# Hybrid NSA and HGRN2 decoder layer: TensorE in a hand-written order through the attention, key blocks two by two

## The chip, the cores and the metric

The kernel runs on one core of a Trainium2 chip. The metric is the device time of one execution in microseconds (us). The core has a matrix engine (TensorE, PE in the profile; PEld are its weight loads), a vector engine (VectorE, DVE), a scalar engine (ScalarE, ACT), GpSimd (POOL) and SyncE (SP), which issues the DMAs. Each engine works through its own instructions in order and waits at semaphores for the others.

## What is computed

One decoder layer for 1024 tokens of width 1024, in float32. The part that matters here is the attention of 8 heads in 2 groups, in query blocks of 128, with three branches whose results are added with gates:

```python
# one query block; R = 4 heads to a group, dh = 64
sc = einsum('bqgrd,bngd->bgrqn', qblk, kc) * scale          # 63 compressed keys
p_cmp = masked_softmax(sc, ...); o_cmp = p_cmp @ vc
ss = einsum('bqgrd,bgqkd->bgrqk', qblk, k_sel) * scale       # selected blocks: 16 of 16, so all earlier keys
p_sel = masked_softmax(ss, ...); o_sel = p_sel @ v_sel
sw = einsum('bqgrd,bkgd->bgrqk', qblk, k_win) * scale        # a window of 512
p_win = masked_softmax(sw, ...); o_win = p_win @ v_win
o = g0 * o_cmp + g1 * o_sel + g2 * o_win
...
x = x + concat(o_nsa, o_hgrn) @ w_out
```

Before it stand a projection and a gated linear recurrence (HGRN2) with 4 heads of its own; after it stands a SwiGLU feed-forward part.

## The kernel before

A product of two float32 operands is made of three reduced-precision ones (`mm3`, lines 117 to 120): each operand is split into a high and a low part by one ACT and one DVE instruction. A tile of the output projection (128 tokens by 512 columns) is 4 such triples, 12 matmuls of 512 columns each (`out_tile`, line 491, before the attention's own functions).

The attention (from line 730) goes through 32 units `(qb, g, b)`: 8 query blocks, 2 groups, and b = 0 for all earlier keys, b = 1 for the window. A unit has two halves. `score` (line 815) makes for each of 4 heads the score rows of the query block against all keys of the unit (PE, lines 839 to 842), their maximum (DVE, line 847), the exponential with its sum (ACT, 848), the reciprocal (DVE, 849) and the scaling (POOL, 850). `values` (line 853) goes through the unit's key blocks: 4 transposes of 128 columns bring a block of the weights into PSUM (line 861), ACT and DVE split it into `ph` (863, 864), and two matmuls of 512 columns add it to the output bank (865, 866). After b = 1, `finish` adds the compressed branch in the same way (872 to 879), folds the halves together (ACT 885 and 886, DVE 887 and 888) and writes the result over the queries. The program calls `score` of one unit ahead of `values` of the unit before it.

`prep` (line 773) serves one query block ahead: POOL scales the queries (775), 8 transposes bring both groups into two PSUM banks (781), ACT and DVE empty each into `q` (784, 785), 16 small matmuls and 2 mask matmuls make the compressed scores (790, 795), and a short softmax follows (803 to 813).

PSUM in this stage: two banks named T for everything that is transposed (`ps_t`), one bank a0 for the unit's output, one bank a1 for output tiles (`bank_f`), and for scores either four single banks (query blocks 0 to 3) or two pairs (`ps_s`, from block `NARROW` = 4).

Output tiles are called between units by a counter: each unit adds 1 plus its number of key blocks to `load`, and each 6.5 (`FILL`) pays for one tile, 12 of the HGRN half first (`hq`), then those of the attention half (`nq`). `out_half(0)` loads the second half of the weights where the first list is empty.

What sets the order: the kernel is written with the Tile framework, which takes the program in order as a priority and orders every engine's instructions itself, by its own model of durations; what is ready may be taken ahead of what stands earlier in the program and isn't.

Of the kernel before, what the change touches and what calls it, by code (L numbers as in the profile page):

```python
# [8 lines left out]
F32 = mybir.dt.float32  # L9
# [39 lines left out]
def hybrid_layer(ctx: ExitStack, tc: tile.TileContext, x, x_t, par, w_in, k_norm, pos_k, pos_v,  # L49
# [441 lines left out]
    def out_tile(parts, t, n, mh, ml, bank):  # L491
        sl = slice(n * 512, (n + 1) * 512)
        a = bank()
        for c in range(4):
            wh, wl = parts[c]
            mm3(a, mh[:, c * P:(c + 1) * P], ml[:, c * P:(c + 1) * P], wh[:, sl], wl[:, sl], c == 0, c == 3)
        V.tensor_tensor(x1[:, t, sl], a, x1[:, t, sl], op=OP.add)
# [7 lines left out]
    mixed = {}  # L505
# [8 lines left out]
    def hgrn_out(t, n, bank=bank_f):  # L514
        if n == 0 and t:
            mixed[t] = mix_parts(gmix[:, :, t * P:(t + 1) * P])
        out_tile(w_b, t, n, *mixed[t], bank)


    with tc.tile_pool(name="cp", bufs=1) as cp:  # L520
# [166 lines left out]
        mixed[0] = mix_parts(gmix[:, :, 0:P])  # L687
# [42 lines left out]
    with tc.tile_pool(name="at", bufs=1) as at:  # L730
        g_bc = at.tile([P, D], F32, name="g_bc")
        nc.sync.dma_start(g_bc, norm_ffn[0:1, :].broadcast_to([P, D]))
        def nsa_out(t, n):
            if n == 0:
                mixed[t] = mix_parts(qtok[:, t].rearrange("p (c n) -> p c n", c=4))
            out_tile(w_t, t, n, *mixed[t], bank_f)
            if n == 1:
                nc.sync.dma_start(x1_d[t * P:(t + 1) * P, :], x1[:, t, :])
                rs2 = norm_stats(x1[:, t, :], rpage())
                if t == NT - 1:  # L740
                    g_last = rpage()
                    nc.sync.dma_start(g_last, norm_ffn[0:1, :].broadcast_to([P, D]))
                    V.scalar_tensor_tensor(x1[:, t, :], x1[:, t, :], rs2, g_last, op0=OP.mult, op1=OP.mult)
                    return
                A.activation(x1[:, t, :], x1[:, t, :], AF.Copy, scale=rs2)
                G.tensor_tensor(x1[:, t, :], x1[:, t, :], g_bc, op=OP.mult)
                if t >= 4:
                    G.tensor_tensor(x1[:, t, 0:512], x1[:, t, 0:512], x1[:, t - 4, 0:512], op=OP.subtract)
# [23 lines left out]
        def prep(qb):  # L772
# [5 lines left out]
            for g in range(GROUPS):  # L778
# [7 lines left out]
                qs.append(q)  # L786
            sc = bank_s() if qb <= NARROW else ps_s()[:, 0:512]
# [26 lines left out]
            return qs, pc3  # L814

        def score(qb, g, b, qs):
# [4 lines left out]
            res = []  # L821
            for r in range(4):
                h = 4 * g + r
                s = bank_s() if qb < NARROW else ps_s()
# [18 lines left out]
                nm = small.tile([P, 1], F32, name="nm", tag="nm", bufs=4)  # L843
                den = small.tile([P, 1], F32, name="den", tag="den", bufs=4)
                p0 = 1024 * r if b == 0 else 4096 + 640 * r
                pp = pflat[:, p0:p0 + n]
                V.tensor_reduce(nm, sv, axis=AX.XY, op=OP.max, negate=True)  # L847
                A.activation(pp.rearrange("p (i n) -> p i n", i=sv.shape[1]), sv, AF.Exp, bias=nm, accum_out=den)  # L848
                V.reciprocal(den, den)  # L849
                G.tensor_scalar(pp, pp, den, gates[:, qb, h * 3 + 1 + b:h * 3 + 2 + b], op0=OP.mult, op1=OP.mult)  # L850
                res.append(pp)
            return kb0, res

        def values(qb, g, b, kb0, wts, o):
            for kb in range(kb0, qb + 1):
                pt = bank_t()

                i = kb - kb0 if b == 0 or qb < 4 else 0 if kb == kb0 else 1 if kb == qb else kb - kb0 + 1
                c0 = i * P
                for r in range(4):  # L860
                    PE.transpose(pt[:, r * P:(r + 1) * P], wts[r][:, c0:c0 + P], ident)  # L861
# [36 lines left out]
        for i, u in enumerate(units + [None]):  # L898
            scored = None
            if u:  # L900
                qb, g, b = u
                if u == (NARROW, 0, 0):
                    paired_banks()
# [394 lines left out]
```

## Time and profile before

| | us |
|---|---|
| median of 3 runs | 1396.63 (1396.52 to 1396.65) |
| the profiled execution: its own time | 1396.95 |
| its span, first to last instruction | 1395.2 |
| attention, from the first query transposes' inputs to the last output products | 392.7 to 745.8 |
| PE busy over the span | 1366.1 (98%) |
| DVE, ACT, POOL busy over the span | 1034.3, 596.7, 322.2 |

PE's busy time counts each matmul from its start to a modelled end. Matmuls overlap in the engine, so one that starts late can still touch the one before it, and the engine counts as busy. How much work was really done is read from starts: how far apart they are, and how many fall into a stretch.

### The profile page before, as it was taken

The page shows a single profiled execution, that of the slowest core. Times are in us where ns is not written, and L with a number is a line of the kernel's source. Part 1 is how long each engine was busy: PE and PEld are TensorE (multiplying, and loading weights), DVE is VectorE, ACT ScalarE, POOL GpSimd, SP SyncE. Part 2 cuts the span into 40 slices and gives each one's busy share as a digit, 9 for nine tenths or more (in the row PEclk, how much of TensorE's full clock was granted, in tenths as well). Part 3 has the DMA queues.
Part 4 walks back from the last instruction along what each step waited for, and adds up shares of the span by engine and source line. Part 5 has one row for each costly group of instructions (what it writes and reads, how often), then busy time and mean ns, then how long its engine had stood idle before and what let it go on. Part 6 is the DMA issues. An engine that isn't in the chain of part 4 may idle for free.

```text
span 1395.2 us, 19645 instructions
## 1 busy us (share of the span) xinstructions
PE 1366.1 (98%) x7092; PEld 1127.8 (81%) x7092; DVE 1034.3 (74%) x1937; ACT 596.7 (43%) x1153; POOL 322.2 (23%) x297
## 2 busy tenths in 40 slices
PE   9999999999999999999998999999999999999998
PEld 7888888989977777777776788888888888888887
DVE  5317888626688887888867888888888887578764
ACT  7323333323446666566664433333333333444432
POOL 0001111011035443344345533323323320000000
PEclk9999999999999999999999999999999999999999
DMA  8411110111220001000003233333233336998521
GB/s 326 128 46 31 31 31 29 54 31 46 76 106 1 1 1 61 31 16 16 31 17 106 70 112 99 113 114 113 92 113 98 114 98 234 335 327 317 180 94 53
DMA packets 108768, 135.71 MB, mean 97 GB/s; under 512 B 6112, under 2 KB 63872, under 8 KB 108672
## 3 DMA queue, kind: packets, MB, share of 16 engines
q1 hardware_dynamic: 108672, 134.46, 28.6%
q8 instruction: 56, 0.92, 0.3%
q14 instruction: 40, 0.33, 0.1%
HBM read 105.87 MB, written 28.57 MB: 96 GB/s over the span
## 4 chain that ended last, share of the span: by engine, by line
PE 85%; DVE 10%; ACT 2%; issue 1%; POOL 1%; DMA 0%; ACTq 0%; POOLq 0%; DVEq 0%
PE bank L118 9%; PE bank L119 9%; PE bank L120 9%; PE a L118 8%; PE a L120 8%; PE a L119 8%; PE ps_t L120 4%; PE ps_t L119 4%; PE ps_t L118 4%; PE ps_t L861 3%; PE a L865 2%; PE a L866 2%; PE ps_t L375 1%; PE ps_s L839 1%; DVE nm L847 1%
## 5 line engine op out<-in xcount | busy, mean ns | idle before, releaser
L111 ACT ACTIVATE wop<-rpage 128x512 fp32r<-128x512 f32 x132 | 82.7, 630 | 156.8 <-PE bank L120 70.6
L850 POOL TENSOR_SCALAR pbig<-pbig,den,gates 128x640 f32<-128x640 f32 (+7 forms) x128 | 104.0, 817 | 167.0 <-DVE den L849 147.0
L112 DVE TENSOR_TENSOR wop<-rpage,wop 128x512 fp32r<-128x512 f32 x132 | 101.4, 771 | 13.4 <-ACT wop L111 11.3
L864 DVE TENSOR_TENSOR ph<-ps_t,ph 128x512 fp32r<-128x512 f32 x126 | 84.4, 684 | 18.5 <-ACT ph L863 17.6
L863 ACT ACTIVATE ph<-ps_t 128x512 fp32r<-128x512 f32 x126 | 72.7, 595 | 49.6 <-PE ps_t L861 38.7
L861 PE MATMUL ps_t<-ident,pbig 128*128 128x128 f32 x504 | 78.7, 275 | 2.1 <-POOL pbig L850 2.1
L381 POOL TENSOR_TENSOR kp<-kp,fp 128x256 f32<-128x256 f32 x28 | 20.3, 726 | 231.8 <-PE bank L358 180.3
L861 PEld LDWEIGHTS ps_t<-ident,pbig 128*128 128x128 f32 x504 | 61.0, 141 | 11.9 <-POOL pbig L850 3.2
L112 DVE TENSOR_TENSOR wlo<-wraw,whi 128x1024 fp32r<-128x1024 f32 (+2 forms) x27 | 32.0, 1188 | 46.2 <-PE a L120 19.3
L848 ACT ACTIVATE pbig<-ps_s,nm 128x640 f32<-128x640 f32 (+3 forms) x64 | 55.9, 875 | 24.1 <-DVE nm L847 19.0
L118 PE MATMUL bank<-wop 128*128 128x512 f32 x165 | 64.2, 389 | 0.0
L119 PE MATMUL bank<-wop 128*128 128x512 f32 x165 | 64.2, 389 | 0.0
L120 PE MATMUL bank<-wop 128*128 128x512 f32 x165 | 64.2, 389 | 0.0
L1012 POOL TENSOR_TENSOR tmp<-tmp,rpage 128x512 f32<-128x512 f32 x21 | 31.2, 1488 | 139.2 <-DVE wop L112 139.2
L111 ACT ACTIVATE wop<-act_a 128x512 fp32r<-128x512 f32 x48 | 30.3, 631 | 73.8 <-PE bank L120 48.3
L847 DVE TENSOR_REDUCE nm<-ps_s 128x1 f32<-128x640 f32 (+3 forms) x64 | 58.1, 914 | 4.7 <-PE ps_s L842 3.0
L865 PE MATMUL a<-ph,kv 128*128 128x512 f32 x132 | 58.8, 446 | 2.3 <-ACT ph L863 1.6
L866 PE MATMUL a<-ph,kv 128*128 128x512 f32 x132 | 57.5, 435 | 2.9 <-DVE ph L864 2.4
L112 DVE TENSOR_TENSOR wop<-tmp,wop 128x512 fp32r<-128x512 f32 x42 | 43.7, 1039 | 20.6 <-ACT wop L111 19.7
L111 ACT ACTIVATE wop<-tmp 128x512 fp32r<-128x512 f32 x42 | 26.6, 634 | 70.1 <-POOL tmp L1012 37.5
L112 DVE TENSOR_TENSOR wop<-act_a,wop 128x512 fp32r<-128x512 f32 x48 | 33.2, 691 | 30.7 <-ACT wop L111 30.6
L118 PE MATMUL a<-whi,hT_h 128*128 128x256 f32 (+2 forms) x168 | 55.2, 328 | 0.0
(458 smaller groups left out, 4352.3 us busy)
## 6 DMA issues: line engine op xcount, KB each, us to landing
rpage<-in_w_gate_up_dram SPq DMA_DIRECT2D x86, 256.0 KB, 3.1
raws<-in_w_down_dram SPq DMA_DIRECT2D x35, 512.0 KB, 7.5
act_a<-act_d SPq DMA_DIRECT2D x12, 1024.0 KB, 6.1
act_d<-as SPq DMA_DIRECT2D x33, 256.0 KB, 2.2
act_e<-act_d SPq DMA_DIRECT2D x6, 1024.0 KB, 8.2
act_d<-tmp SPq DMA_DIRECT2D x22, 256.0 KB, 2.2
act_d<-th SPq DMA_DIRECT2D x22, 256.0 KB, 2.1
xn<-in_x_dram SPq DMA_DIRECT2D x8, 512.0 KB, 6.0
```

The source lines that it names most:

```text
L111: A.activation(hi, src, AF.Copy)
L112: V.tensor_tensor(lo, src, hi.bitcast(F32), op=OP.subtract)
L118: PE.matmul(o, ah, bh, start=first, stop=False, skip_group_check=chained)
L119: PE.matmul(o, ah, bl, start=False, stop=False, skip_group_check=chained)
L120: PE.matmul(o, al, bh, start=False, stop=last, skip_group_check=chained)
L847: V.tensor_reduce(nm, sv, axis=AX.XY, op=OP.max, negate=True)
L850: G.tensor_scalar(pp, pp, den, gates[:, qb, h * 3 + 1 + b:h * 3 + 2 + b], op0=OP.mult, op1=OP.mult)
L861: PE.transpose(pt[:, r * P:(r + 1) * P], wts[r][:, c0:c0 + P], ident)
L863: A.activation(ph[:, 0], pt, AF.Copy)
L864: V.tensor_tensor(ph[:, 1], pt, ph[:, 0].bitcast(F32), op=OP.subtract)
L865: PE.matmul(o, vst[b][:, kb, g, :], ph[:, 0], start=b == 0 and kb == kb0, stop=False)
L866: PE.matmul(o, vst[b][:, kb, g, :], ph[:, 1], start=False, stop=False)
```

## The change

Within the attention loop PE's instructions keep the order in which the program issues them (`tc.manual_schedule` with PE alone). The other engines are still ordered by the framework. To have an order worth keeping, the work is cut into pieces:

- an output tile becomes 4 pieces of 3 matmuls (`out_pieces`);
- `score` gives back 4 closures, one for each head, with an estimated cost;
- `values` and `finish` give back steps of three parts: `turn` (transposes and splits), `first` and `second` (the two products);
- `run_steps` takes a unit's steps two by two: both `turn`s, then as many heads and pieces as make an equal share of the unit's fills, then `first`, `first`, `second`, `second`;
- the order in a unit is now: steps of the unit before, with this unit's heads and pieces between them;
- `prep` is cut in two: its 8 transposes come ahead of the steps of unit (qb, 1, 1), and the compressed scores are a fifth "head" of that unit (`later_weights`);
- two products of the feed-forward part (`first_pieces`) become fills of the last steps, and the last output tiles come after them.

```diff
-    def out_tile(parts, t, n, mh, ml, bank):
+    def out_pieces(parts, t, n, mix, bank, tail=None):
...
+        def piece(c):
+            def run():
+                if c == 0:
+                    a.append(bank())
+                wh, wl = parts[c]
+                mh, ml = mix
+                mm3(a[0], mh[:, c * P:(c + 1) * P], ml[:, c * P:(c + 1) * P], wh[:, sl], wl[:, sl], c == 0, c == 3)
+                if c == 3:
+                    V.tensor_tensor(x1[:, t, sl], a[0], x1[:, t, sl], op=OP.add)
+                    if tail:
+                        tail()
+            return run
+        return [piece(c) for c in range(4)]
...
                 qs.append(q)
+            return qs, lambda: compressed(qb, qs)
+
+        def compressed(qb, qs):
             sc = bank_s() if qb <= NARROW else ps_s()[:, 0:512]
...
+            cost = 0.16 + 0.9 * max(n, 256) / 1024
+            return kb0, res, [(lambda r=r: head(r), cost) for r in range(4)]
 
         def values(qb, g, b, kb0, wts, o):
-            for kb in range(kb0, qb + 1):
+
+            def step(kb):
+                ph = []
+
+                def turn():
+                    pt = bank_t()
...
+                    for r in range(4):
+                        PE.transpose(pt[:, r * P:(r + 1) * P], wts[r][:, i * P:(i + 1) * P], ident)
+                    ph.append(at.tile([P, 2, 512], F32R, name="ph", tag="ph", bufs=2))
+                    A.activation(ph[0][:, 0], pt, AF.Copy)
+                    V.tensor_tensor(ph[0][:, 1], pt, ph[0][:, 0].bitcast(F32), op=OP.subtract)
+
+                def first():
+                    PE.matmul(o, vst[b][:, kb, g, :], ph[0][:, 0], start=b == 0 and kb == kb0, stop=False)
+
+                def second():
+                    PE.matmul(o, vst[b][:, kb, g, :], ph[0][:, 1], start=False, stop=False)
+                return turn, first, second
+            return [step(kb) for kb in range(kb0, qb + 1)]
...
+        def run_steps(steps, fills):
+
+            pairs = [steps[k:k + 2] for k in range(0, len(steps), 2)]
+            todo, share = list(fills), sum(c for _, c in fills) / max(len(pairs), 1)
+            used = 0.0
+            for k, pair in enumerate(pairs):
+                for turn, _, _ in pair:
+                    turn()
+                while todo and (k == len(pairs) - 1 or used + todo[0][1] / 2 < share * (k + 1)):
+                    used += todo[0][1]
+                    todo.pop(0)[0]()
+                for j in (1, 2):
+                    for st in pair:
+                        if st[j]:
+                            st[j]()
+            for f, _ in todo:
+                f()
...
+        with tc.manual_schedule(engines={mybir.EngineType.PE}):
+            for i, u in enumerate(units + [None]):
+                scored, heads, fills, steps, ahead = None, [], [], [], []
+                if u:
...
+                    kb0, res, heads = score(qb, g, b, prepped[qb][0])
...
+                while load >= FILL:
+                    load -= FILL
+                    if hq:
+                        t, n = hq.pop(0)
+                        if n == 0:
+                            ahead.append(lambda t=t: hgrn_mix(t))
+                        fills += [(f, 0.7) for f in hgrn_pieces(t, n, bank_f, None if hq else half)]
...
+                if i == len(units):
+                    for t in nq:
+                        fills += nsa_fills(*t)
+                    nq = []
+                    for f in range(2):
+                        fills += first_pieces(f)
+                if u and u[1:] == (1, 1) and u[0] + 1 < NT:
+                    prepped[u[0] + 1] = prep(u[0] + 1)
+
+                    def later_weights(q=u[0] + 1):
+                        compr[q] = prepped[q][1]()
+                    heads.append((later_weights, 2.3))
...
+                    steps = values(qb, g, b, kb0, wts, o_bank[g])
+                    if b == 1:
+                        steps.append(finish(qb, g, compr[qb], o_bank[g]))
...
+                for _ in range(EARLY.count(i - len(units))):
...
+                    steps.append((lambda t=b11_t: operand(b11, x1[:, t, 0:512], t, ps_t), None, None))
+                    b11_t += 1
+
+                k = len(heads) > 3 and len(steps) > 4
+                for f in ahead:
+                    f()
+                run_steps(steps, heads[:2] + fills[:1] * k + heads[2:] + fills[k:])
...
+            mixed[NT - 1] = []
+            nsa_mix(NT - 1)
+            for t in nq:
+                for piece in nsa_pieces(*t):
+                    piece()
```

## Rows read from the trace of the kernel before

**Rows 1.** Busy time by stretch: window and length, each engine's busy us (instructions), PEclk.
```profile
392.70:518.00 125.30, 121.81 (x755) 96.82 (x755) 101.72 (x258) 78.87 (x215) 56.79 (x77) 0.99 0.02 5
518.00:745.80 227.80, 219.28 (x1235) 171.18 (x1235) 181.82 (x387) 142.00 (x279) 86.84 (x75) 0.99 0.08 29
597.60:627.60 30.00, 29.55 (x177) 24.00 (x177) 26.25 (x58) 19.80 (x40) 12.59 (x12) 1.00 0.04 18
```
**Rows 2.** Instructions of one line in the attention: count, duration min/median/max, stretch, forms.
```profile
L861 PE MATMUL ps_t<-ident,pbig x504: 270/272/421, 400.8 to 733.3; 128*128 128x128 f32 x168
L861 PE MATMUL ps_s<-ident,pbig x24: 270/272/299, 718.2 to 733.0; 128*128 128x128 f32 x24
L118 PE MATMUL a<-whi,rpage x108: 387/397/775, 394.5 to 744.4; 128*128 128x512 f32 x108
L839 PE MATMUL ps_s<-kv,q x128: 277/388/522, 504.1 to 717.5; 128*128 128x384 f32 x48, 128*128 128x256 f32 x32, 128*128 128x320 f32 x16, 128*128 128x448 f32 x16
L839 PE MATMUL bank<-kv,q x64: 279/380/562, 395.8 to 495.2; 128*128 128x256 f32 x32, 128*128 128x384 f32 x16, 128*128 128x512 f32 x16
```
**Rows 3.** Timeline of PE where nothing waits: start, us, engine, line, operation, tiles, count.
```profile
570.37 0.39 PE L119 MATMUL a<-wlo,rpage 128*128 128x512 f32 x1
570.60 0.39 PE L120 MATMUL a<-whi,rpage 128*128 128x512 f32 x1
...
571.18 0.28 PE L839 MATMUL ps_s<-kv,q 128*128 128x256 f32 x1
571.30 0.28 PE L840 MATMUL ps_s<-kv,q 128*128 128x256 f32 x1
...
571.90 1.04 PE L861 MATMUL ps_t<-ident,pbig 128*128 128x128 f32 x8
572.69 0.48 PE L118 MATMUL a<-whi,rpage 128*128 128x512 f32 x1
```
**Rows 4.** Timeline around the query transposes of block 3, all engines.
```profile
462.77 0.93 PE L781 MATMUL ps_t<-ident,rpage 128*128 128x128 f32 x7
...
463.45 0.48 PE L118 MATMUL a<-whi,rpage 128*128 128x512 f32 x1
...
463.76 1.27 ACT L784 ACTIVATE q<-ps_t,gains 128x512 fp32r<-128x512 f32 x2
...
464.65 1.41 DVE L785 SCALAR_TENSOR_TENSOR q<-ps_t,gains,q 128x512 fp32r<-128x512 f32 x2
```
**Rows 5.** Timeline of one head of block 0, from its mask matmul to its scaled weights.
```profile
400.41 0.23 PE L842 MATMUL bank<-cmask,identb 128*128 128x128 bf16 x1
...
400.67 0.29 DVE L847 TENSOR_REDUCE nm<-bank 128x1 f32<-128x128 f32 x1 [0.31 <-PE bank L842]
...
401.73 1.37 POOL L850 TENSOR_SCALAR pbig<-pbig,den,gates 128x128 f32<-128x128 f32 x3 [1.19 <-DVE den L849]
```
**Rows 6.** Groups by line and form, heads of 640 keys and the block split: count | busy, mean ns.
```profile
L847 DVE TENSOR_REDUCE nm<-ps_s 128x1 f32<-128x640 f32 x40 | 32.2, 813 | 2.7 <-PE ps_s L840 1.4 <-PE ps_s L842 1.1
...
L848 ACT ACTIVATE pbig<-ps_s,nm 128x640 f32<-128x640 f32 x40 | 31.7, 794 | 12.6 <-DVE nm L847 10.7 <-DVE den L849 1.6 <-DVE n_rs L131 0.2
...
L850 POOL TENSOR_SCALAR pbig<-pbig,den,gates 128x640 f32<-128x640 f32 x40 | 37.1, 929 | 74.5 <-DVE den L849 63.0 <-PE ps_s L840 10.7 <-DVE n_rs L131 0.6
...
L864 DVE TENSOR_TENSOR ph<-ps_t,ph 128x512 fp32r<-128x512 f32 x126 | 84.4, 684 | 18.5 <-ACT ph L863 17.6
...
L863 ACT ACTIVATE ph<-ps_t 128x512 fp32r<-128x512 f32 x126 | 72.7, 595 | 49.6 <-PE ps_t L861 38.7 <-issue 4.4 <-PE a L866 1.9
```
**Rows 7.** Busy time by stretch again: before and in a stretch of lower granted clock.
```profile
420.80:424.20 3.40, 1.75 (x14) 1.28 (x13) 2.57 (x9) 3.01 (x12) 3.40 (x5) 1.00 0.00 0
424.20:427.60 3.40, 3.40 (x14) 2.83 (x14) 3.06 (x10) 2.37 (x9) 2.08 (x5) 0.50 0.01 2
```
**Rows 8.** Timeline at the end of the attention: last compressed product, last split.
```profile
737.75 0.29 PE L879 MATMUL a<-ph,vc_up 128*128 128x256 f32 x1
...
740.30 0.69 DVE L511 TENSOR_TENSOR rpage<-qtok,rpage 128x512 fp32r<-128x512 f32 x1
```

More of the change, by code (lines that the diff above doesn't have):

```diff
@@ L503, in bank_f @@
         return ps.tile([P, 512], F32, name="a1", tag="a1", bufs=1)
-    mixed = {}
+    mixed = {t: [] for t in range(NT)}
     def mix_parts(src):
@@ L842, in score @@
                         PE.matmul(s[:, o0 + mo:o0 + mo + wm], identb, cmask[:, m0 + 256 - wm:m0 + 256], start=False, stop=True)
[L843 to L852, printed above, removed]
-        def values(qb, g, b, kb0, wts, o):
-            for kb in range(kb0, qb + 1):
-                pt = bank_t()
[L858 to L861, printed above, removed]
-                ph = at.tile([P, 2, 512], F32R, name="ph", tag="ph", bufs=2)
-                A.activation(ph[:, 0], pt, AF.Copy)
-                V.tensor_tensor(ph[:, 1], pt, ph[:, 0].bitcast(F32), op=OP.subtract)
-                PE.matmul(o, vst[b][:, kb, g, :], ph[:, 0], start=b == 0 and kb == kb0, stop=False)
-                PE.matmul(o, vst[b][:, kb, g, :], ph[:, 1], start=False, stop=False)
@@ L868, in finish @@
[L868 to L875 removed]
+                softmax(r, sv)
@@ new lines, in finish, with turn @@
+        def finish(qb, g, pc3, o):
+            ph = []
+            def turn():
+                pt = bank_t()
+                for k in range(2):
+                    h = 4 * g + 2 * k
+                    PE.transpose(pt[:, k * P:(k + 1) * P], pc3[:, h:h + 2, :].rearrange("p h n -> p (h n)"), ident)
+                ph.append(at.tile([P, 2, 512], F32R, name="ph", tag="ph", bufs=2))
+                A.activation(ph[0][:, 0, 0:256], pt[:, 0:256], AF.Copy)
+                V.tensor_tensor(ph[0][:, 1, 0:256], pt[:, 0:256], ph[0][:, 0, 0:256].bitcast(F32), op=OP.subtract)
@@ L882, in finish, with fold @@
+            return turn, lambda: product(0), second
+        def fold(qb, g, o):
             mix = qtok[:, qb].rearrange("p (c n) -> p c n", c=4)
@@ L937, in hybrid_layer, with half, nsa_fills @@
-        first = [product(qtok[:, f], b11, at.tile([P, 2, 512], F32R, name="wop0", tag="q", bufs=3), ps_t())
-                 for f in range(2)]
-        for t in nq:
-            nsa_out(*t)
+        w_t, load = [], 0
+        def half():
+            w_t.extend(out_half(0))
+        def nsa_fills(t, n):
+            if n == 0:
+                mixed[t] = []
+                ahead.append(lambda: nsa_mix(t))
+            return [(f, 0.7) for f in nsa_pieces(t, n)]
+        b11, b11_t, first = None, 0, []
```

160 lines of the change are left out of this document (82 added, 78 removed).

## The prediction

> **What bounds the kernel now.** I read the busy table first (PE 98% of the span), then the busy times by stretch, because the change touches only the attention, 392.7 to 745.8 us, then starts of matmuls. In [rows 1] PE is busy for 121.81 of 125.3 us and 219.28 of 227.8 us: by this view 12 us are free. That view hides short waits, since a matmul that starts late still overlaps the one before. So I count instead. Where nothing waits, matmuls of 512 columns start 0.23 us apart, those of 256 columns 0.12 us, and the 8 transposes take 0.11 us each ((1.04 - 0.27) / 7) [rows 3]. The counts [rows 2], completed from the code: 655 transposes (528 of them on line 861); 676 matmuls of 512 columns (line 118's 108 and 8 of the feed-forward part, each three times, 132 each on lines 865 and 866, and 16 on each of lines 839 and 840 for both kinds of bank); of 384, 256, 448 and 320 columns, 128, 192, 32 and 32; and 272 small ones (compressed scores and masks), priced as transposes. That gives 72.1 + 155.5 + 22.4 + 23.0 + 6.4 + 4.8 + 29.9 = 314 us of work (between 256 and 512 columns in proportion). The stage takes 353 us, so PE loses about 39 us in waits, nearly all of them short. Counted likewise, some 12 of these fall before 518 us (blocks 0 to 3) and 27 after. This is all that a better order can win, and VectorE sets a floor below it: in unit group (5, 1) it is busy for 26.25 of 30.0 us [rows 1], where PE's work is about 27.
>
> **What the change does to PE's waits.** The instructions are the same. A fixed order has no cover beyond what it places, so I go through it unit by unit, and list the places at which the next PE instruction cannot be ready. The new sum of waits stands against the 39 us.
>
> *Pairs.* From the first transpose of a pair: the first block is transposed after 0.6 us (3 x 0.11 + 0.27), ACT takes 0.595 us for each block and VectorE 0.684 us [rows 6], so ACT is done at about 1.2 and 1.8, VectorE at 1.9 and 2.6. PE has spent 0.87 us on 8 transposes and needs the second block's low part 0.7 us after its fills. A pair with 1.0 us of fills or more thus waits for nothing if ACT and VectorE are free. From the code I counted 80 pairs; most have 1.4 to 2.8 us of fills. This is the good part of the change. But heads make VectorE late by up to 0.81 us [rows 6], so I leave 0.1 us a pair: 8 us. Bounds: 0.03 (2 us) and 0.25 (20 us, the present waits per block).
>
> *Thin pairs.* Units (1, 1, 0), (3, 1, 0) and (7, 0, 1) have pairs with 0.6 to 0.8 us, one with none, because their counter pays for no tile: 0.3 to 1.0 us each, 3 us together.
>
> *Softmax of the last head.* The next unit begins with transposes that need all four heads' weights. Where the last head stands at a unit's end with no tile behind it, PE waits. From a mask matmul at 400.41 to the end of the scaling at 401.73 + 1.37 the trace shows 2.7 us for 128 keys [rows 5]; for 640 keys maximum, exponential and scaling alone take 0.81 + 0.79 + 0.93 = 2.5 us [rows 6]; with the sum, the reciprocal and the passing on I estimate 3.1. In the program of before the next unit's scores run in that time; in the new order they are queued behind the waiting transposes, so VectorE's next maxima are late as well. What PE still has: its own mask matmul (0.1), and products. Unit (0, 0, 0): 2.6 us wait; (0, 0, 1): 2.7 less queueing and 0.6, 1.6; (1, 0, 0): 1.8; (2, 0, 0): 2.2; (7, 0, 1), whose last step has no products: 3.1. Together 11.3 us; bounds 8 and 14.
>
> *The query transposes.* Seven times 8 transposes fill both T banks right ahead of a pair that needs both. For block 3 [rows 4] the transposes start at 462.77 and end at 463.4, and ACT and VectorE empty the banks by 465.36 and 466.06 (the half and the end of 1.41 us). Before, PE goes on at 463.45 with a tile's matmul. In the new order nothing but transposes into those banks comes next: it waits until 465.36, and 0.3 us more for the second bank, 2.2 us. Queued behind it on PE are the unit's own heads, for which VectorE and then POOL wait in turn. Without the fold that holds ACT until 463.76 it would be about 1.3. I take 1.9: 13.3 us; bounds 9 and 16.
>
> *Pairs of score banks.* From block 4 on two score tiles are in flight. In units (4, 1, 1) and (5, 1, 1) the third head follows the first after one head and one piece (1.4 us), and the compressed scores come right behind the fourth; a maximum and an exponential of 640 keys take 1.6 us [rows 6] besides the passing on: 0.4 + 1.0 us twice, 2.8 us; bounds 0 and 5.
>
> *Second half of the output weights.* Their 8 splits now have most of a unit between the last HGRN piece and the first that needs them; I leave 1 us.
>
> *The end.* Before, the feed-forward products cover the fold of the last unit, which runs from 737.75 + 0.29 to 740.99 [rows 8]. The new order spends them before that, and PE has about 3 us with nothing of the attention; what follows may move up. I take the middle, 1.5 us.
>
> *The clock.* Twice the granted clock falls to 0.5, that is from 2.4 to 1.2 GHz; the first time from 424.2 to 427.6 us, right after a stretch in which PE was busy for 1.75 of 3.4 us, and 14 matmuls ran in it [rows 7]. If PE is kept busy through such a stretch at half speed it loses up to 1.7 us. The new order has waits of 1.6 to 3 us in at least five places, so I count four such stretches at 1.2 us: 4.8 us, bounds 0 and 13. The Trainium skill warns of this: the page "TensorE: Matmul & The Clock Gate", section "A second HAM failure mode: psum-queue depth-cycling", says that short idles between groups of matmuls, made by cycling through PSUM banks, can make the clock swing and cost throughput. By that rule every one of the 12 bank and softmax waits above would bring a low stretch; the trace, with two low stretches beside many more waits, bears it out only for the long ones.
>
> The sum: 8 + 3 + 11.3 + 13.3 + 2.8 + 1 + 1.5 + 4.8 = 45.7 us of waits against 39, which is 6.7 us more: 1396.95 + 6.7 = 1403.7 for the profiled execution, which stands 0.3 above the median, so 1403.3. Its own range, with the pair term at 0.05 to 0.15 us and the query term at its ends: 1398 to 1409. Other stages aren't touched. The DMAs that the moved steps issue (the residual rows to memory, the weights' second half, the gains) come from the same places of the program and keep their order on SP; POOL's query scaling still comes ahead of the unit's own scalings.
>
> **Rivals.** *The order wins.* While PE waits at a query transpose, ACT and VectorE work off what would have delayed the next pairs; then the pairs cost nothing (2 us), each query transpose 1.3 (9 us), the thin pairs and score banks 2, the softmax waits 9, and with shorter waits there are two low stretches (3 us). 25 us of waits against 39: 1396.95 - 14 - 0.3 = 1383; with half of that gain, 1390; I give 1387 as its time. For it speaks that PE loses 39 us in short waits which most pairs would cover; against it that the new waits stand at known places. It decides where the waits not listed by place (the 8 us) come out below 1.
>
> *VectorE becomes the bound.* With 26.25 of 30.0 us busy [rows 1] and a fixed PE order, each late split stops PE. At 0.25 us a pair the term is 20 instead of 8: 1415.
>
> *The clock falls at every bank wait.* The seven query transposes, the five softmax waits and the two thinnest units bring a low stretch of 1.2 us each: 17 instead of 4.8, 1415. The rule of the Trainium skill named above would have it so.
>
> *Nothing changes.* The framework's order may already be about as good, waits only change places: 1396.6.
>
> **How the numbers follow.** The forecast (slower by 3 to 12 us) 0.40, the order wins 0.36, nothing changes 0.15, VectorE 0.05, the clock 0.04. So slower 0.49, faster 0.36, same 0.15, where 0.2% (2.8 us) is about what a measurement of this kernel can tell from no change. The range takes in the winning order at 1385 and nearly all of the worse cases: 1385 to 1414.
>
> **What would show it.** In the profile after: PE idle ahead of line 861 or its successor in seven places just behind the query transposes, released by VectorE's `q`; waits of 2 to 3 us ahead of the transposes in units (0, 0, 1), (0, 1, 0), (1, 0, 1), (2, 0, 1) and (7, 1, 0), released by POOL's scaling; hardly any wait ahead of the products; low clock in more than two stretches. The stage should take about 360 us. I am wrong if the products' waits stay (then VectorE), if the listed places show under 20 us, or if the stage takes under 350.

## The result, and the profile after

| | before | after |
|---|---|---|
| median of the runs, us | 1396.64 | 1459.1 (1455.06 to 1464.64) |
| ratio | | 1.045 [1.0395, 1.0506] |
| profiled execution's span, us | 1395.2 | 1462.9 |
| attention stage in it, us | 392.7 to 745.8 (353) | 393 to 806 (413) |
| mean granted clock of that execution | 0.997 | 0.976 |

The change makes the kernel 4.5% slower. One of the four runs of the kernel before took 1502.94 us, far above the other three (1396.5 to 1396.7), and the ratio leaves it out. 60 of the 67.7 us by which the span grew lie in the attention. The page of the changed kernel, PE's busy time and its clock (in 40 slices):

```profile
PE 1392.2 (95%) x7092; PEld 1151.6 (79%) x7092; DVE 1043.1 (71%) x1937; ACT 596.6 (41%) x1153; POOL 319.7 (22%) x297
...
PEclk9999999999978999999998899999999999999999
```

The count of matmuls is unchanged, and at full clock none has got dearer by itself (a transpose of a key block has a median of 0.27 us in both). VectorE's and ScalarE's busy times are within 1% of those before, over a longer span. The stretches show where the rate was lost (window: length, each engine's busy us and instructions, PEclk, DMA share, GB/s):

```profile
400.00:500.00 100.00, 86.06 (x457) 67.57 (x457) 63.84 (x175) 48.95 (x145) 34.66 (x54) 0.85 0.00 1
500.00:600.00 100.00, 89.70 (x507) 71.56 (x506) 74.32 (x144) 56.22 (x124) 31.33 (x36) 0.95 0.08 24
600.00:700.00 100.00, 90.27 (x526) 72.33 (x525) 78.18 (x167) 60.96 (x124) 40.73 (x36) 1.00 0.05 19
700.00:800.00 100.00, 84.06 (x428) 65.80 (x426) 65.64 (x149) 51.46 (x96) 30.09 (x25) 0.91 0.05 22
```

From 400 to 500 us PE starts 457 matmuls, and its granted clock is 0.85. In the kernel before, the same hundred microseconds have 592 and 0.98; [rows 1] show the stage as a whole:

```profile
400.00:500.00 100.00, 96.85 (x592) 75.92 (x591) 81.20 (x219) 66.69 (x190) 47.63 (x69) 0.98 0.00 1
```

Of PE's waits from 393 to 840 us the view of waits lists these first (what PE waited in, for which engine's result: us in total, times, longest us):

```profile
PE ps_t L892 <- DVE q L805: 14.0, 7, 3.0
PE ps_s L874 <- ACT pbig L853: 12.1, 10, 3.6
PE ps_t L892 <- POOL pbig L855: 8.5, 9, 1.8
PE a L901 <- DVE ph L895: 4.8, 12, 1.2
PE a L898 <- ACT ph L894: 3.5, 5, 1.8
```

Line 892 is the transposes of a key block (861 before), 874 the scores of a head (839), 898 and 901 the two products (865, 866), 805 the low part of the queries (785), 853 the exponential (848), 855 POOL's scaling (850). In the kernel before, the longest entry of this view for the stage has 3.5 us:

```profile
PE ps_s L839 <- ACT pbig L848: 3.5, 7, 0.9
```

As the prediction did, I also count by starts: each start of a matmul against the spacing of its form in [rows 3]. What exceeds it is a wait; in stretches of lower clock the excess goes to the clock, up to once the spacing. The window goes from 393 us to 590 us before the last instruction, so it holds the same work in each kernel (some 60 us of it feed-forward, with 8 us of waits in every kernel). The work is 364 us in both kernels, within 2.4 us. The rest, also for the experiments:

| kernel | median us | waits us | lost to the clock us | us at low clock |
|---|---|---|---|---|
| before | 1396.6 | 45.8 | 3.0 | 6.8 |
| after | 1459.1 | 86.1 | 27.3 | 68.3 |
| e1: query transposes into score banks | 1457.9 | 88.2 | 17.3 | 44.4 |
| e2: unread matmuls in the waits | 1453.4 | 83.9 | 12.9 | 34.1 |
| e4: a head ahead of each unit | 1452.1 | 83.7 | 23.9 | 54.6 |
| e5: last unit's banks | 1456.7 | 85.1 | 19.7 | 47.8 |
| e6: key blocks one by one | 1518.1 | 146.0 | 20.4 | 51.2 |
| e7: heads and pieces alternate | 1474.7 | 99.6 | 18.2 | 44.4 |
| e13: three mends together | 1435.3 | 76.3 | 11.3 | 27.3 |
| e9: pieces free | 1430.1 | 69.1 | 9.7 | 23.9 |
| e10: scores free | 1419.1 | 60.3 | 10.1 | 23.9 |
| e11: pieces and scores free | 1394.8 | 40.8 | 4.5 | 10.2 |
| e12: all free, one by one | 1401.6 | 46.9 | 5.5 | 13.7 |
| e3: all free | 1391.8 | 38.3 | 2.7 | 6.8 |
| e14: all free, with e13's mends | 1389.0 | 37.1 | 2.6 | 6.8 |

From before to after 40.3 us of waits and 24.3 us of clock, with the 2.4 us, are 67.0 of the 67.7 us.

The medians come from all executions, the other columns from the profiled one alone. For the changed kernel that was the slowest of four: 1464.6 us at a mean granted clock of 0.976, where two others took 1455.1 us at 0.984 and 0.985. By the table's price (27.3 us for 68.3 us of low clock) a difference of 0.009 in the clock, 26 us of low clock, is an estimated 10 us. So the changed kernel's loss to the clock is an estimated 17 to 27 us, by execution, and a difference in clock between it and an edited kernel can be chance up to that size.

Two kinds of wait can be seen in the timelines. Behind the query transposes of block 3, the place of [rows 4] (start, us, engine, line, tiles; in brackets the idle time before and what ended it):

```profile
483.62 1.04 PE L801 MATMUL ps_t<-ident,rpage 128*128 128x128 f32 x8
...
484.61 1.27 ACT L804 ACTIVATE q<-ps_t,gains 128x512 fp32r<-128x512 f32 x2
...
485.51 1.41 DVE L805 SCALAR_TENSOR_TENSOR q<-ps_t,gains,q 128x512 fp32r<-128x512 f32 x2
...
486.41 1.22 PE L892 MATMUL ps_t<-ident,pbig 128*128 128x128 f32 x8 [1.75 <-DVE q L805]
```

In [rows 4] a tile's matmul starts 0.68 us after the first of the seven transposes shown there; here nothing follows until VectorE has emptied the first T bank. In the last unit (7, 1, 1) a wait on score banks:

```profile
764.74 0.60 PE L892 MATMUL ps_s<-ident,pbig 128*128 128x128 f32 x4
...
765.71 0.34 PE L875 MATMUL ps_s<-kv,q 128*128 128x384 f32 x1
...
766.18 0.68 DVE L522 TENSOR_TENSOR rpage<-qtok,rpage 128x512 fp32r<-128x512 f32 x1
...
767.09 0.69 DVE L895 TENSOR_TENSOR ph<-ps_s,ph 128x512 fp32r<-128x512 f32 x1 [0.17 <-ACT ph L894]
...
767.76 0.82 DVE L852 TENSOR_REDUCE nm<-ps_s 128x1 f32<-128x640 f32 x1
...
768.67 0.79 ACT L853 ACTIVATE pbig<-ps_s,nm 128x640 f32<-128x640 f32 x1 [1.61 <-DVE n_rs L127]
769.61 0.58 PE L874 MATMUL ps_s<-kv,q 128*128 128x256 f32 x1 [3.56 <-ACT pbig L853]
```

The transposes of a key block sit in one of the two score pairs (`ps_s` as the target of line 892), so the next head needs the pair of the head whose scores end at 766.05. Its maximum starts 1.7 us after that, since VectorE is still busy with the operand of an output tile (line 522) and with the split of a key block (895). PE, which may take nothing else, stands for 3.56 us.

### The profile page after: what moved, and what is told of

It reads as the page before. It is cut to its first block, busy times and chain, and to the rows that moved or that the text cites. A ratio compares the mean times of both kernels' runs of the same rounds, so it can differ in the third digit from the quotient of the medians.

```text
span 1462.9 us, 19612 instructions
## 1 busy us (share of the span) xinstructions
PE 1392.2 (95%) x7092; PEld 1151.6 (79%) x7092; DVE 1043.1 (71%) x1937; ACT 596.6 (41%) x1153; POOL 319.7 (22%) x297
## 4 chain that ended last, share of the span: by engine, by line
PE 80%; DVE 12%; ACT 3%; issue 2%; POOL 1%; DMA 0%; ACTq 0%; SPq 0%; POOLq 0%; DVEq 0%
PE bank L118 9%; PE bank L119 9%; PE bank L120 9%; PE a L118 8%; PE a L120 8%; PE a L119 8%; PE ps_t L118 4%; PE ps_t L119 4%; PE ps_t L120 4%; PE ps_t L892 3%; DVE ph L895 2%; PE a L901 2%; DVE nm L852 2%; PE ps_t L375 1%; PE a L898 1%
## 5 line engine op out<-in xcount | busy, mean ns | idle before, releaser
L855 POOL TENSOR_SCALAR pbig<-pbig,den,gates 128x640 f32<-128x640 f32 (+7 forms) x128 | 100.6, 792 | 214.9 <-DVE den L854 203.9
L874 PE MATMUL ps_s<-kv,q 128*128 128x384 f32 (+4 forms) x128 | 51.9, 407 | 12.3 <-ACT pbig L853 12.1
L901 PE MATMUL a<-ph,kv 128*128 128x512 f32 x132 | 50.7, 432 | 5.5 <-DVE ph L895 4.8
L120 PE MATMUL a<-whi,hT_l 128*128 128x256 f32 (+2 forms) x168 | 55.0, 327 | 0.0
```

The source lines that it names most:

```text
L120: PE.matmul(o, al, bh, start=False, stop=last, skip_group_check=chained)
L901: PE.matmul(o, vst[b][:, kb, g, :], ph[0][:, 1], start=False, stop=False)
```

## The experiments

Each was run against the kernel before on the same chip. My theory after the first look: the pieces of the program are sound, and what costs is that the order is written by hand, since behind a wait PE finds only what was written there. Rivals: a few badly chosen places; the clock; the cutting of the program itself.

**Order or program (e3, e8).** The changed program without its fixed order, and the kernel before with one.

```diff
-        with tc.manual_schedule(engines={mybir.EngineType.PE}):
+        with ExitStack():
```

> The changed program, cut into the same pieces in the same order, but without the fixed order of PE: the framework orders PE as in the kernel before. If the fixed order costs the time, this comes back to 1395 to 1410, with a low clock for under 15 us. If the new cut and program order cost it (other priorities for ACT, VectorE and POOL), it stays above 1435.

1391.8 us (1390.29 to 1392.77), ratio 0.9965 [0.9951, 0.9979]: 0.35% faster than before, and a little below the expected range. The cutting costs nothing; the loss is the order. After the query transposes of block 3 PE now has this:

```profile
458.67 0.27 PE L801 MATMUL ps_t<-ident,rpage 128*128 128x128 f32 x1
458.70 0.37 PE L922 MATMUL a<-ph,vc_st 128*128 128x256 f32 x1
458.90 0.28 PE L922 MATMUL a<-ph,vc_up 128*128 128x256 f32 x1
459.02 0.93 PE L801 MATMUL ps_t<-ident,rpage 128*128 128x128 f32 x7
459.70 0.42 PE L875 MATMUL bank<-kv,q 128*128 128x384 f32 x1
```

Products of the unit before stand between them, and all heads of the new unit behind them.

```diff
+        fixed = tc.manual_schedule(engines={mybir.EngineType.PE})
+        fixed.__enter__()
...
+        fixed.__exit__(None, None, None)
```

> One part of the change alone: the kernel before, with PE held to the program's order in the attention loop, and nothing cut or interleaved. Each key block then waits for its own split: about 1.9 us from the first transpose to the low part, of which 0.44 us are transposes and 0.23 us the first product, so some 1.2 us lost for each of 148 blocks, 175 us, and a low clock through most of the stage, another 50 us or more: 1590 to 1680. If holding the order costs little in itself, it stays under 1480.

1766.9 us, ratio 1.265, far above both expected ranges. PE waits for the split at almost each of the 132 blocks (here the view of the whole execution, since the stage lasts beyond 1100 us):

```profile
PE a L865 <- ACT ph L863: 108.3, 129, 2.3
PE ps_s L839 <- ACT pbig L848: 22.9, 17, 2.7
```

Counted by starts as above, it has some 270 us of waits and loses some 140 us to the clock, which is granted at 0.87 on the mean. So the change's interleaving by hand is worth 308 us against a plain written order (1766.9 - 1459.1), and the framework's own interleaving, which the kernel before had already, 370 us.

**Two by two (e6, e12).** Key blocks singly, in the written order and in a free one.

```diff
-            pairs = [steps[k:k + 2] for k in range(0, len(steps), 2)]
+            pairs = [steps[k:k + 1] for k in range(len(steps))]
```

> One edit to the changed kernel: key blocks one by one instead of two by two, each with its share of heads and pieces between its transposes and its products. A block's low part is ready about 1.9 us after its first transpose, and a share is now about 1.1 us, so if cover decides, waits ahead of the products grow by 0.2 to 0.4 us a block, 148 blocks: 1480 to 1510, with more low clock. If the bursts of two blocks are what makes ACT and VectorE late, the waits for banks and softmax shrink and it comes to 1440 to 1455.

1518.1 us, ratio 1.0872 [1.0854, 1.089], just above the range for cover, and with the waits ahead of the products that it foretold:

```profile
PE a L901 <- DVE ph L895: 26.7, 72, 1.5
PE a L898 <- ACT ph L894: 22.8, 36, 2.4
```

> The changed program with no fixed order, and its key blocks written one by one instead of two by two. It tells whether writing two by two is what makes the freely ordered form 0.35% faster than the kernel before. Theory A (without a fixed order the framework makes its own interleaving and the written pairs hardly matter): within 3 us of 1391.8 us. Rival B (the pairs are the gain): 1396 us or more, as the kernel before, and the products' waits grow by about 5 us.

1401.6 us, ratio 1.0032 [1.0019, 1.0045]. Against after and e3, writing two by two gains 59 us in the written order and about 10 us in the free one. Here theory A fell: what is written is the framework's priority, and with pairs in it the result is faster. Without them the re-cut program is slower than the kernel before, so the pairs are also why e3 beats it.

**Single places (e1, e4, e5, e7).** The query transposes into score banks:

```diff
+            sp = None if qb <= NARROW else ps_s()
...
-                pt = bank_t()
+                pt = bank_s() if sp is None else sp[:, 512 * g:512 * (g + 1)]
```

> One edit to the changed kernel: the query transposes of a block go into a score bank (a score pair from block 5 on) instead of the two T banks, so the pair behind them finds its banks free. If the waits behind the query transposes cost what the trace of the changed kernel shows (14.0 us in 7 waits) and a share of the low clock comes with them, the time falls by 15 to 22 us, to 1436 to 1446, and the wait on line 892 for VectorE's q disappears. If these waits only give ACT and VectorE time that they need anyway, the same time comes back ahead of the pairs' products and the kernel stays at 1452 to 1464.

1457.9 us (1457.65 to 1465.38). The 14 us behind the T banks are gone, and the total is the same: the transposes now wait longer for POOL (11.6 us instead of 8.5), the compressed scores for a score bank (line 814), and from block 5 on the second half of the query transposes waits until VectorE has emptied the first half of the same score pair (line 802), which is this edit's own cost.

```profile
PE ps_t L893 <- POOL pbig L856: 11.6, 13, 1.7
PE ps_s L875 <- ACT pbig L854: 11.1, 9, 3.6
PE ps_s L802 <- DVE q L806: 6.3, 3, 2.1
...
PE bank L814 <- ACT pbig L854: 4.8, 4, 1.7
```

The last unit's transposes kept out of the score pairs:

```diff
-                free[0] = i >= len(units) - 1
+                free[0] = i >= len(units)
```

> One edit to the changed kernel: only the step behind the last unit, not the last unit itself, may use a score pair for its transposes, so the last unit's heads keep both score pairs. The trace of the changed kernel shows waits of 3.6 and 2.6 us there ahead of line 874 for ACT's exponential. If that bank is the cause, both go and the time falls by 6 to 10 us, to 1446 to 1456; if VectorE and ACT are late there anyway, the waits stay and so does the time.

1456.7 us (1453.57 to 1457.73), just above the expected range.

```profile
PE ps_s L874 <- ACT pbig L853: 5.0, 7, 1.7
```

The waits of line 874 fall from 12.1 to 5.0 us, and the longest from 3.6 to 1.7, which shows that the transposes in a score pair made the long ones; 2.2 us come up at line 898 (5.7 instead of 3.5). Of the 7 us only 1 is left in the sum of waits (86.1 to 85.1). One head ahead of each unit's first transposes:

```diff
             for k, pair in enumerate(pairs):
+                if k == 0 and todo:
+                    used += todo[0][1]
+                    todo.pop(0)[0]()
```

> One edit to the changed kernel: in each unit the first head's scores come ahead of the first two blocks' transposes instead of behind them. If the waits stand at the unit starts because nothing may run there (14.0 us behind the query transposes, 8.5 us for POOL's scaling in the trace of the changed kernel), a head of 0.4 to 1.05 us covers a part of each of 16 waits and some low clock goes with them: 8 to 16 us faster than the changed kernel, 1443 to 1451. If ACT and VectorE are late through the whole stage, the waits move to the products and it stays at 1452 to 1462.

1452.1 us (1448.04 to 1455.99), the lowest median of the single edits, but between the two expected ranges, and not for the reason expected. The waits at the unit starts hardly shrink (14.0 to 12.6 us and 8.5 to 7.2); those of line 874 do (12.1 to 4.8):

```profile
PE ps_t L892 <- DVE q L805: 12.6, 7, 2.8
PE ps_t L892 <- POOL pbig L855: 7.2, 8, 1.8
...
PE ps_s L874 <- ACT pbig L853: 4.8, 5, 2.6
```

Heads and pieces in turn:

```diff
-                run_steps(steps, heads[:2] + fills[:1] * k + heads[2:] + fills[k:])
+                spread = []
+                for n_ in range(max(len(heads), len(fills))):
+                    spread += heads[n_:n_ + 1] + fills[n_:n_ + 1]
+                run_steps(steps, spread)
```

> One edit to the changed kernel: heads and pieces alternate one to one in each unit, so that two heads never follow each other while pieces last. If the waits ahead of line 874 come from two heads too close for two score tiles, they fall from 12.1 us to under 7 us; the last head then comes later in the unit and the wait for POOL's scaling grows from 8.5 to some 14 us: 1453 to 1464 in all. If spreading also helps ACT and VectorE, both fall and it comes under 1450.

1474.7 us (1468.55 to 1475.44), above both expected ranges. Line 874 leaves the list of the longest waits, since heads are no longer close together; but the last head comes later, and the next unit waits for its softmax:

```profile
PE ps_t L892 <- POOL pbig L855: 29.1, 24, 3.0
```

Of these edits only e7 changes the time clear of noise. The ratios of e1, e4 and e5 to the kernel before (1.0451, 1.0397, 1.0426) have intervals that overlap with the changed kernel's own [1.0395, 1.0506]. What these three show is which waits move, and that the sum of waits hardly changes.

**The clock (e2).** Matmuls whose result nobody reads, in the waits:

```diff
+        def dummies(n):
+            o = bank_f()
+            for _ in range(n):
+                PE.matmul(o, identb, cmask[:, 0:512], start=True, stop=True)
...
+                    dummies(7)
...
+                if i in (1, 2, 5, 9, 30):
+                    dummies(5)
```

> No wait is removed. Where the changed kernel waits longest, 7 matmuls of 512 bf16 columns whose result nobody reads are put in: behind the query transposes of 7 units, and 5 each ahead of the first transposes of five units that wait for the softmax of the unit before. If the long waits bring the granted clock down, and the low clock costs about 23 us, the low time falls from some 45 to 70 us to under 30 and the kernel gets faster by 8 to 15 us although it does more work. If the waits alone cost the time and the clock is a side effect, it stays at 1455 to 1464 or gets a few us slower.

1453.4 us (1450.29 to 1458.3), a smaller gain than the 8 to 15 us expected, and with an interval of its ratio (1.0386 to 1.0432) that overlaps with the changed kernel's. The wait for the queries is now filled:

```profile
PE ps_t L892 <- DVE q L805: 3.4, 7, 1.5
```

In the profiled executions the time at low clock halves (68.3 to 34.1 us). Over all four executions of each kernel the difference is smaller: mean granted clocks of 0.984 to 0.991 here, 0.976 to 0.985 in the changed kernel. That low clock costs time is clearer in the changed kernel alone: the same program took 9.6 us more at 0.976 than at 0.985. So the clock is a price on top of the waits, and matmuls in the waits bring some of it back; with at most 27.3 of 67.7 us it is not the main cause.

**What must be free (e9, e10, e11).** Parts of the changed program taken out of the fixed order one after the other; the others stay in it.

```diff
+        def loose(run):
+            def free_run():
+                fixed[0].__exit__(None, None, None)
+                run()
+                hold()
+            return free_run
...
-                        fills += [(f, 0.7) for f in hgrn_pieces(t, n, bank_f, None if hq else half)]
+                        fills += [(loose(f), 0.7) for f in hgrn_pieces(t, n, bank_f, None if hq else half)]
```

> The changed kernel, with only the pieces of output tiles outside the fixed order: scores, query transposes, compressed scores, transposes and products of the key blocks keep the order written for TensorE among themselves, and the framework places the pieces. Theory A (the fixed order is slow because TensorE cannot take ready work of later units while it waits; the pieces, some 100 us of matmuls, are ready early and would fill): most of the 67 us between the changed kernel and its freely ordered form comes back, 1400 to 1425 us, with the waits behind the query transposes and the softmax under 12 us together (22.5 in the changed kernel) and the granted clock of the span above 0.99. Rival B (scores and transposes themselves stand in a bad order, and pieces cannot mend that): above 1440 us, and the waits of the transposes (line of the turns) keep 20 us or more.

> The changed kernel, with only the scores of heads and the compressed scores outside the fixed order: transposes, products and pieces of output tiles keep the written order. Theory A: scores can now run ahead into an earlier wait, so the transposes that wait for the softmax (8.5 us) and the scores that wait for their banks (12.1 us) lose most of that, and the query transposes have work behind them; 1415 to 1440 us. Rival B (transposes and products set the time): 1445 us or more, with the waits of the products unchanged or longer.

> Scores and pieces both outside the fixed order; only the query transposes, the transposes and the products of the key blocks, two by two, and the last steps keep the written order among themselves. Theory A: nearly as the freely ordered form, 1392 to 1405 us. Rival B (it is the order of transposes before products, pair by pair, that costs): 1430 us or more.

1430.1 us (1427.65 to 1434.03), 1419.1 us (1417.46 to 1420.12) and 1394.8 us (1392.38 to 1395.69; ratio to before 0.9983 [0.9973, 0.9993]). Against the 1459.1 us that is 29, 40 and 64 of the 67 us that separate the written order from the free one. Free pieces came out 5 us above my range, the other two within theirs; to free the scores as well brings another 35 us. In the traces of the first and the third the instructions left fixed keep their order but for a few. In the second some pieces move too: 49 of the 336 matmuls of pieces in the stage, most of them in its first 60 us, start earlier among the transposes and products than written, so a part of its 40 us may be theirs. The waits of the first lines with pieces free, then with scores free, then with both:

```profile
PE ps_s L874 <- ACT pbig L853: 8.2, 5, 3.3
PE ps_t L892 <- POOL pbig L855: 5.7, 14, 0.8
PE a L898 <- ACT ph L894: 5.5, 9, 1.2
PE ps_t L892 <- DVE q L805: 5.4, 4, 2.0
```

```profile
PE a L901 <- DVE rs_t L126: 3.3, 3, 2.1
PE ps_s L874 <- ACT pbig L853: 2.9, 5, 1.3
```

```profile
PE bank L742 <- POOL d L1119: 2.7, 1, 2.7
PE ps_t L892 <- POOL pbig L855: 2.2, 5, 1.3
```

With both free the longest is one of the feed-forward part, 2.7 us, which the changed kernel has too. The order of transposes before products, two by two, which is the idea of the change, may stay fixed at a cost of some 3 us (1394.8 against 1391.8, from different comparisons and with overlapping intervals of the ratios). What cost the time was the fixed place of the fillers, that is of heads and pieces.

**Mends together (e13, e14).** Two pieces and two heads behind the query transposes, one head ahead of every other unit, and no transposes in a score pair while there are scores to come:

```diff
-                free[0] = i >= len(units) - 1
+                free[0] = i >= len(units)
...
-                run_steps(steps, heads[:2] + fills[:1] * k + heads[2:] + fills[k:])
+                lead = heads[:1]
+                if len(heads) > 4 and fills:
+                    lead = fills[:1] + heads[:1] + fills[1:2] + heads[1:2]
+                for f, _ in lead:
+                    f()
+                later = heads[:2] + fills[:1] * k + heads[2:] + fills[k:]
+                run_steps(steps, [p for p in later if p not in lead])
```

> The changed kernel, TensorE still wholly in a written order, with the places mended that the trace names: behind the query transposes stand two pieces of an output tile and two heads before the next transposes, every other unit begins with one head, and the last units keep the score banks to the scores. Theory A (the waits stand at a few places of the written order, and a better written order is as good as a free one): the mends add up, 14 us behind the query transposes, 5 to 10 us at score banks and softmax and 5 to 10 us of clock go; 1420 to 1432 us. Rival B (each mend moves its wait to another place, as the single mends did, because the work placed there is missing elsewhere): 1440 us or more, the wait of the transposes for the query parts under 4 us but the waits of the products over 15 us.

1435.3 us (1433.72 to 1436.56), between the two theories.

```profile
PE a L898 <- ACT ph L894: 7.6, 11, 1.5
PE ps_t L892 <- POOL pbig L855: 7.3, 9, 2.6
PE ps_s L874 <- ACT pbig L853: 6.4, 13, 1.7
```

The waits for the queries are gone from the head of the list, and 24 of the 67 us are back. Between the two profiled executions it is 28 us, 16 of them clock and 10 waits, where a part of the clock is due to the low clock of that one execution of the changed kernel. But the products' waits by starts rise from 15.6 us (lines 898 and 901) to 23.2, as they would if the fillers spent behind the queries were missing between the pairs. So both theories hold in part. A better written order exists; whether one as good as the free order can be written was not tried further.

> The same program as the mended one, with no fixed order for TensorE. It tells whether the order in which the program is written still matters once the framework orders TensorE. Theory A (it hardly does; only the writing two by two did): within 3 us of 1391.8 us. Rival B: the written order steers the framework too, and the mends help or hurt by more than 3 us.

1389.0 us (1388.32 to 1389.35), ratio 0.995 [0.9934, 0.9967]: the fastest of all, 7 us below the kernel before and 2.8 us below e3, which is at the edge of what the two theories allowed. The two ran in different comparisons, so that the mends help here as well is likely rather than shown.

## Why the prediction was right or wrong

The direction was right (slower, given 0.49). The size was not: the forecast had +6.7 us, the range ended at 1414, and 1459.1 is far outside. The step that failed is the new sum of waits, 45.7 us set against 39: it went through listed places and took what could not be listed as nearly nothing, and it counted on the pairs to replace the present waits. The sum came to about 113 us by the same count (86.1 of waits and 27.3 of clock, some 8 of them in the feed-forward part). Most of what was missing is in three terms: the clock, the score banks and the pairs. Even the sign was in part luck, since the two terms that held, the first two below, make 24.6 us and the sum beat the 39 us only by terms that were mis-sized.

Two of the prediction's own figures do not follow from its terms. With the pair term and the query term at the ends given, the forecast runs from 1395 to 1410, not from 1398 to 1409; and the 25 us of *The order wins* leave out the 2.5 us for the weights' second half and the end. Neither reaches 1459.

Term by term, measured by starts in the same lines:

| term | predicted us | measured us |
|---|---|---|
| query transposes | 13.3 | 15 (14.0 in the view of waits, 7 times) |
| softmax of the last head | 11.3 | 15 (8.5 in the view, 9 times) |
| pairs and thin pairs | 11 | 19.9 (lines 898, 901 and 922) |
| pairs of score banks | 2.8 | 18.2 (line 874, and 813 and 818) |
| weights' second half, the end | 2.5 | 5.2 (line 118) |
| clock | 4.8 | 27.3 |

*Right:* the query transposes. Seven waits, five of them of 1.75 us against 1.9 estimated from [rows 4]; e1 showed that the T banks make them, though their time came back elsewhere. For the softmax, four of the five listed places show a wait: by starts 1.6 us in unit (0, 0, 1), 2.2 in (1, 0, 1), 3.5 in (7, 1, 0) in two parts, but only 1.1 in (2, 0, 1). (0, 1, 0) shows none, and (1, 1, 0), which wasn't listed, 1.5; some 5 us are waits under 0.4 us. These two terms could be read from before, because each is one chain of known operations [rows 4 to 6].

*Mis-sized, the clock:* four stretches were counted, and the price was about right: 1.2 us for each 3.4 us, where 27.3 us for 68.3 us of low clock make 1.36. The count failed: there were 11 low stretches with 58 us in the stage, and 10 us behind it. I took [rows 7] to mean that only the longest waits matter, and priced the other case at 0.04. Two waits of the changed kernel with what follows, at the query transposes of block 1 and of block 5:

```profile
412.40:416.40 4.00, 1.03 (x10) 0.81 (x9) 3.22 (x9) 2.85 (x10) 1.77 (x3) 1.00 0.00 0
416.40:420.00 3.60, 3.59 (x20) 3.22 (x20) 2.33 (x9) 1.91 (x7) 0.45 (x1) 0.56 0.02 5
...
570.80:574.20 3.40, 1.65 (x14) 1.35 (x13) 2.25 (x4) 2.02 (x4) 0.00 (x0) 0.95 0.36 114
574.20:577.60 3.40, 3.40 (x17) 3.21 (x16) 2.19 (x3) 1.19 (x2) 0.00 (x0) 0.55 0.10 40
```

With 1.75 us of wait the clock can fall as it does with 3. Within 1.6 us of the end of a query wait it fell at blocks 1, 2, 4 and 5, and it didn't at blocks 3, 6 and 7. The Trainium skill (the page "TensorE: Matmul & The Clock Gate", section "A second HAM failure mode: psum-queue depth-cycling") says that frequent small idles between groups of matmuls make the clock go to and fro. The trace agrees in that the clock fell 11 times in the stage, but not for every wait (three of the seven query waits had no fall). My own figure for that rival, 17 us, was nearer than the forecast's 4.8.

*Mis-sized, the score banks:* I looked for pairs only in the units where a third head follows closely, and found two. But the score lines were not free before: by the same count lines 839, 840, 790 and 795 lost some 10 to 12 us of the 39, and nothing in the change removed them. I overlooked that with the last unit's heads moved between the transposes of the unit before, `bank_t`, which is unchanged, puts transposes into a score pair while heads still need it (e5: 7 us of line 874's waits). And I took the maximum and the exponential as starting at once, where VectorE's other work held the first for 1.7 us.

*Wrong, the pairs:* What I called the good part of the change was set against 39 us of present waits as if it would replace them. Lines 865 and 866 had 14.1 us before, 898 and 901 have 15.6 after. Pairs do work (e6), but the framework had covered most of the splits already: the kernel before, held to its plain written order, waits 108.3 us at line 865 (e8). So the new waits at listed places were not paid for by any gain: that is the step from which the sign followed more clearly than I gave it.

*What would show it:* the seven query waits and the low clock in more than two stretches came out. "Hardly any wait ahead of the products" did not, nor the stage of about 360 us (413). The largest gap after the clock is that of the score banks, 15.4 us. The sign that I gave for VectorE as the bound, that the products' waits stay, did come out, but the rival has no support: VectorE is busy 63.84 of 100 us from 400 to 500 in the changed kernel, 81.20 before. The sign did not tell the two apart.

## What to carry to other kernels

Before an engine's order is fixed by hand, the same program should be timed with the order left to the framework: here the re-cut program was 0.35% faster than before (0.5% with the mends), and holding TensorE to the written order made it 67 us slower. If an order is to be fixed, fix only the dependent chain (transposes, then products, in pairs) and leave the fillers free: that cost some 3 us here, and fillers moved by hand to one wait seemed to be missing at the next (e13). And a wait that is added on TensorE should be priced with the clock that may follow it: in the profiled execution of the changed kernel 40 us more of waits came with 24 us more of clock. Last, single mends are best judged by the sum of waits and not by the wait that they remove: here most of each wait that went came back elsewhere.

## What the runs showed of the hardware that I had not expected

Waits of the same length are followed by a lower clock at one place and not at another. At the query transposes of block 3 PE waits 1.75 us, is busy for 1.65 of 3.4 us, and keeps its full clock:

```profile
483.60:487.00 3.40, 1.65 (x15) 1.26 (x13) 2.25 (x4) 2.02 (x4) 3.00 (x3) 1.00 0.00 0
487.00:490.40 3.40, 3.22 (x25) 2.46 (x24) 2.69 (x7) 2.25 (x5) 0.30 (x1) 1.00 0.00 0
```

At block 5, with the same wait and the same 1.65 us of work in 3.4 us, the granted clock is 0.55 in the stretch after it (above), that is most of it at 1.2 instead of 2.4 GHz. What decides between the two isn't shown here. The changed kernel's own spread goes with it: its four executions took 1455.1 to 1464.6 us, at mean granted clocks of 0.985 down to 0.976.
